# A hybrid decoder layer on one core: the first merge branch's weights in other buffers, its layer norm steps held back, and the memory stage's parts and stores in another order

## The chip, the cores and the metric

The kernel runs on one core of a Trainium2 chip. The metric is the time of one execution on the device, in microseconds (us). Before the change the median of three runs is 1679.34 us (1675.44 to 1679.78).

The engines are named as the profile names them: PE multiplies matrices (PEld loads its weights), DVE, ACT and POOL work element by element, and SP issues most of the transfers.

## The reference

The layer takes 1024 tokens of width 1024, in float32:

```
xn   = RMSNorm(x)
proj = xn @ w_in      # columns: attention q | 6 x k/v | gates | conv (2 x 512) | memory q (512) | 3 x 1024 merge gates
A: o_nsa  = sparse attention, 8 heads of 64: compressed blocks + top-16 selected blocks + window of 512
B: u      = silu(LayerNorm(causal depthwise conv, width 31, of a * sigmoid(ag)))
C: o_mem  = softmax(qm km^T / sqrt(128)) vm, 4 heads of 128 over 256 memory tokens
merged = sigmoid(g0) * (o_nsa @ w_nsa_out) + sigmoid(g1) * (u @ w_conv_out) + sigmoid(g2) * (o_mem @ w_mem_out)
h      = x + merged @ w_out
out    = h + (silu(hn @ w_gate) * (hn @ w_up)) @ w_down,   hn = RMSNorm(h)
```

With 1024 tokens the 16 selected blocks of 64 are all blocks, so branch A needs no gather: it is masked softmaxes over the compressed blocks, the keys and the window.

## The kernel before

**Products in parts.** Almost every product of float32 matrices is made of three. Each operand is split (`split`, lines 130 to 132) into a high part, which ACT casts (line 131), and a low part, the source less the high part, which DVE or, in places, POOL subtracts (line 132). `mm3` (line 153) then adds high by high, high by low and low by high into one bank of accumulators (`ps`, seven in three rings, and one bank `pf` for the gates). All of these are line 146 on PE.

**The stages in order.** The program is one sequence of stages for the same 1024 tokens:

1. Input norm, transposes, conv inputs, queries and compression (to about 262 us in the profile).
2. The memory stage. Eight units (2 head pairs by 4 tiles of 256 tokens) in `mem_attention`: scores and softmax (`mem_softmax`; POOL scales by the reciprocals at line 619), a transposition by 32 by 32 squares that goes through DRAM (`mem_squares` stores to `pd`, `mem_load` reads back), and the product with the values (`mem_out`). `mem_out` casts the read probabilities on ACT and subtracts on POOL, as one instruction of 128 by 1024, then makes 12 products of 256 columns for its two heads, and stores the result's parts to `md`. Between these stand the attention's query projections (`queries`). `square_queries` reads the stored queries back, scales them on POOL at line 356, transposes and stores them.
3. The K/V stage (its first PE transposes of keys stand at 387 us): eight projections (`wide_proj`), norm of the keys on DVE and ACT, and `keys(t)`, four PE transposes at line 696 and copies into place. `keys` runs one tile behind the projection. The last `mem_out` stands behind the first projection.
4. The attention (its last waits end at 806 us): for each of 8 token tiles and 2 groups, the scores of a step, masks and softmax, transposes of the probabilities on PE (line 932, and line 918 for the compressed part), their parts (ACT line 131, DVE line 132), and the products with the values. The selected blocks' probabilities go through `wd` in DRAM (line 855 stores 8 pieces per tile and group, line 869 reads).
5. The merge, three branches in the order memory, attention, convolution. For each branch four weight units `w` (512 by 256 columns, split into parts), and for each of 8 column blocks `d_` and 2 halves one bank of 12 products of 512 columns, which is multiplied by the sigmoid of a gate (`zz`, read from `zd`) and added to `acc`. `layer_norm` is a generator: each `next(steps)` runs a piece of the convolution's norm (sums of four, means by a product with `ones` at line 1023, squares, variances at line 1035, scaling, Silu and split), two pieces for each `d_`.
6. Output product, norm and feed-forward part.

**What fills PE.** The convolution's taps (line 445, on DVE) run along stages 2 and 3. The merge gates' projections (bank `pf`, weights in two buffers `fsl` with a staging buffer `fst` of their own) are fillers: the first 12 of 24 column blocks are free, and the others are tied one by one to matmuls of the attention. Fillers and taps have a later priority, so a scheduler puts them where the main line waits. What a merge weight needs: a staging buffer `st` (two in the kernel), a buffer for the parts, a load on SP's queue, a cast on ACT and a subtraction on DVE. `anyslab` hands out the part buffers by turns: three `wsl` and two `fsl`. In the attention the `wsl` buffers hold the squares that line 855 stores to `wd`, so a merge weight in one of them can only be cast once those stores have landed.

`follow(m, i)` orders instruction m behind i without data between them.

Of the kernel before, what the change touches and what calls it, by code (L numbers as in the profile page):

```python
# [8 lines left out]
F32 = mybir.dt.float32  # L9
# [3 lines left out]
OP = mybir.AluOpType  # L13
# [4 lines left out]
P = 128  # L18
S = 1024
D = 1024  # L20
NT = S // P
# [18 lines left out]
def hybrid_layer_kernel(  # L40
# [4 lines left out]
    nc = tc.nc  # L45
    x, mem, out = x[0], mem[0], out[0]
# [33 lines left out]
    turn = [0, 0, 0]  # L80
# [18 lines left out]
    def bank(shape, dt=F32, p=P, at=None):  # L99
        if at is None:  # L100
            turn[1] += 1
            at = order[turn[1] % len(order)]
        return psp[at].tile([p] + shape, dt, tag=f"ps{at}", name=nm("ps"))
# [26 lines left out]
    def split(hi, lo, src, eng=None):  # L130
        m = nc.scalar.copy(hi, src)  # L131
        return m, (eng or nc.vector).tensor_tensor(lo, src, hi.bitcast(F32), op=OP.subtract)  # L132
# [20 lines left out]
    def mm3(o, ah, al, bh, bl, start, stop):  # L153
        first = mm(o, ah, bh, start, False)
        mm(o, ah, bl, False, False)
        mm(o, al, bh, False, stop)
        return first
# [48 lines left out]
    def follow(m, i, why):  # L206
        tc.add_manual_dep(m.ins, i.name, ORDER, reason=why)
# [139 lines left out]
        nc.scalar.activation(stat, stat, AF.Sqrt, scale=stat.shape[2] / 512.0, bias=RMS_EPS)  # L347
        nc.vector.reciprocal(stat, stat)

    def square_queries(j, t, stat):  # L350

        h = stat.shape[2]
        raw, sq = t2([512]), t2([512])
        nc.sync.dma_start(raw, qraw[j, t])
        v = raw.rearrange("p (h d) -> p h d", h=h)
        nc.gpsimd.tensor_tensor(v, v, stat[:, t, :, None].to_broadcast([P, h, 512 // h]), op=OP.mult)
        if j == 0:
            nc.vector.transpose(sq.rearrange("p (c h s) -> p h c s", c=4, h=4),
                                raw.rearrange("p (h c s) -> p h c s", h=4, c=4))
            o = qt_m[t].rearrange("c r a x -> r c a x")  # L360
        else:
            for g in range(2):
                nc.vector.transpose(sq.rearrange("p (g c h s) -> p g h c s", g=2, c=2, h=4)[:, g],
                                    raw.rearrange("p (g h c s) -> p g h c s", g=2, h=4, c=2)[:, g])
            o = qt_n[t].rearrange("g c r a x -> r (g c) a x")
        for a in range(4):
            nc.sync.dma_start(o[:, :, a], sq[32 * a:32 * a + 32].rearrange("p (c x) -> p c x", c=4))
# [210 lines left out]
        ps = tok_proj(row_units(w_mem_kv, 512 + hp * 256), 0, mn)  # L578
        split(VM[:, 0, :, hp * 256:(hp + 1) * 256], VM[:, 1, :, hp * 256:(hp + 1) * 256], ps)

    msc, exps = float(P) ** -0.5, []

    def mem_qload(u):
        raw = t2([2, 4, 2, 32])
# [38 lines left out]
    def mem_squares(hp, tp, pm):  # L623
        T_ = t4([2, 4, 2, 2, 32])
        for tt in range(2):
            nc.vector.transpose(T_[:, :, :, :, tt, :].rearrange("p m c h s -> p h (m c) s"),
                                pm[:, tt].rearrange("p h (b s) -> p h b s", s=32))
        for a in range(4):
            nc.sync.dma_start(pd[hp, tp, :, :, :, a, :].rearrange("m c r x -> r (m c) x"),
                              T_[32 * a:32 * a + 32].rearrange("p m c h t s -> p (m c) (h t s)"))  # L630

    def mem_load(hp, tp):
        PT = slab([2, 2, 4, 2, 2, 32])
        nc.sync.dma_start(PT[:, 1].bitcast(F32).rearrange("p m a h t s -> p m (a h t s)"),
                          pd[hp, tp].rearrange("m c r a x -> (c r) m (a x)"))
        return PT

    def mem_out(hp, tp, PT):
        follow(split(PT[:, 0], PT[:, 1], PT[:, 1].bitcast(F32), nc.gpsimd)[0], exps[-1],
               "parts behind the next unit's exponentials")  # L640
        o = bank([2, 256])
        for h in range(2):
            hh = 2 * hp + h
            for mb in range(2):
                ph, pl = (PT[:, hl, mb, :, h].rearrange("p a t s -> p t a s") for hl in range(2))
                mm3(o[:, h, :].rearrange("p (t a s) -> p t a s", t=2, a=4), VM[:, 0, mb, hh * P:(hh + 1) * P],
                    VM[:, 1, mb, hh * P:(hh + 1) * P], ph, pl, mb == 0, mb == 1)
        om = [PT[:, hl, 0].rearrange("p a h t s -> p (a h t s)").rearrange("p (h t) -> p h t", h=2) for hl in range(2)]
        split(om[0], om[1], o)
        for hl in range(2):  # L650
            nc.sync.dma_start(md[2 * hp:2 * hp + 2, :, hl, tp * 256:(tp + 1) * 256].rearrange("h p t -> p h t"),
                              om[hl].bitcast(F32))

    def mem_attention(ws):

        raws, PT = [mem_qload(0), mem_qload(1)], {}
        QM = mem_queries(raws.pop(0))
        for u in range(8):
            if u < 6:
                raws.append(mem_qload(u + 2))  # L660
            pm = mem_softmax(u // 4, u % 4, QM)
            if u < 7:
                QM = mem_queries(raws.pop(0))
            mem_squares(u // 4, u % 4, pm)
            queries(ws, u, 1, rqn)
            if u > 1:
                mem_out(0 if u < 6 else 1, (u - 2) % 4, PT[u - 2])
            if u > 0:
                PT[u - 1] = mem_load((u - 1) // 4, (u - 1) % 4)
            if u == 3:  # L670
                stat_rms(rqn[:, 0:4])
            if u > 3:
                square_queries(1, u - 4, rqn)
        mem_out(1, 2, PT[6])
        return mem_load(1, 3)

    ws = [wide_unit(w_in, C_Q, u, alloc=slab if u == 3 else wslab) for u in range(4)]
    pt3 = mem_attention(ws)
    stat_rms(rqn[:, 4:8])


# [15 lines left out]
        for s in range(2):  # L697
            nc.vector.tensor_copy(key_cols(s, t), b[:, s].bitcast(F32))

    last = None  # L700
    for t in range(NT):
        if t < 4:
            square_queries(1, 4 + t, rqn)
        v = wide_proj(ws, t).rearrange("p (s a g d) -> p s a g d", s=2, a=2, g=2)
        if t == 0:
            mem_out(1, 3, pt3)
        kn = t2([2, 2, 64])
        heads_norm(v[:, :, 0], kn)
        nc.vector.tensor_tensor(kn, kn, gn[:, 2:4, None, :].to_broadcast([P, 2, 2, 64]), op=OP.mult)
        cat = t2([4, 2, 64], F32R)  # L710
        split(cat[:, :, 0, :], cat[:, :, 1, :], kn.rearrange("p s g d -> p (s g) d"))
        for s in range(2):
            split(VSW[s][:, t, :, 0:64], VSW[s][:, t, :, 64:128], v[:, s, 1])
        if last is not None:
            keys(t - 1, last)
        last = cat
    keys(NT - 1, last)


    with low(TAP):  # L720
# [342 lines left out]
    for n_, (br, wt) in enumerate(branches):  # L1063
        ins = nxt
        for dp in range(4):
            w = unit(wt[0, :, dp * 256:(dp + 1) * 256].rearrange("(k p) c -> p k c", p=P), [4, 256], alloc=anyslab)
            if dp == 2 and n_ == 0:
                nxt = [heads_in(k) for k in range(4)]
            elif n_ == 1:
                nxt = conv  # L1070
            for d_ in (2 * dp, 2 * dp + 1):
                for _ in range(2):
                    next(steps, None)
                wc = (d_ % 2) * P
                zz = t4([S])
# [2 lines left out]
                for half in range(2):  # L1078
# [14 lines left out]
                    if n_ == 2:  # L1093
# [2 lines left out]
                        m = MG[half][dp]  # L1096
                        split(m[:, 0, d_ % 2, :], m[:, 1, d_ % 2, :], a)


    def mg(hl, k, half, a, b):  # L1100
        return MG[half][k // 2][:, hl, k % 2, a:b]
# [375 lines left out]
```

## Time and profile before

| | us |
|---|---|
| median of 3 runs | 1679.34 |
| profiled execution, its own time | 1677.4 |
| span of the profiled execution | 1675.4 |
| PE busy in the span | 1637.0 |
| DVE busy | 1063.6 |
| ACT busy | 737.3 |
| POOL busy | 638.9 |
| mean granted clock of PE | 0.995 of full speed |

The span is what the trace covers; the 2.0 us between it and the execution's own time lie around it. "Busy" of PE includes matmuls that run at half the clock; the rows by windows give the granted clock as a share of full speed in their eighth column. The row of a group or a wait names engine, line and tiles; buffer numbers are left out there. In rows of the timeline a bracket gives the idle time ahead of an instruction and what ended it.

### The profile page before, as it was taken

The page shows a single profiled execution, that of the slowest core. Times are in us where ns is not written, and L with a number is a line of the kernel's source. Part 1 is how long each engine was busy: PE and PEld are TensorE (multiplying, and loading weights), DVE is VectorE, ACT ScalarE, POOL GpSimd, SP SyncE. Part 2 cuts the span into 40 slices and gives each one's busy share as a digit, 9 for nine tenths or more (in the row PEclk, how much of TensorE's full clock was granted, in tenths as well). Part 3 has the DMA queues.
Part 4 walks back from the last instruction along what each step waited for, and adds up shares of the span by engine and source line. Part 5 has one row for each costly group of instructions (what it writes and reads, how often), then busy time and mean ns, then how long its engine had stood idle before and what let it go on. Part 6 is the DMA issues. An engine that isn't in the chain of part 4 may idle for free.

```text
span 1675.4 us, 22491 instructions
## 1 busy us (share of the span) xinstructions
PE 1637.0 (98%) x7904; PEld 1368.2 (82%) x7904; DVE 1063.6 (63%) x1796; ACT 737.3 (44%) x1363; POOL 638.9 (38%) x551
## 2 busy tenths in 40 slices
PE   7999999999999999997999999999999999999999
PEld 6887898777888888886788888888888888888887
DVE  6279888798565665666585526865545555466655
ACT  6311344442676766575584324432223223233332
POOL 0010003451367767665115302465566766400000
PEclk9999999999999999999899999999999999999999
DMA  8134456663355555438654224233334445793763
GB/s 286 40 97 119 139 152 178 193 197 118 108 150 167 165 173 163 141 118 290 215 192 155 84 76 139 76 124 95 96 110 141 145 151 188 275 398 118 233 226 125
DMA packets 249430, 266.31 MB, mean 159 GB/s; under 512 B 24084, under 2 KB 173892, under 8 KB 247782
## 3 DMA queue, kind: packets, MB, share of 16 engines
q1 hardware_dynamic: 242406, 252.30, 47.4%
q10 hardware_dynamic: 6912, 12.59, 2.0%
q8 instruction: 62, 1.02, 0.2%
q14 instruction: 50, 0.41, 0.1%
HBM read 184.09 MB, written 80.74 MB: 158 GB/s over the span
## 4 chain that ended last, share of the span: by engine, by line
PE 89%; DVE 4%; DMA 3%; issue 2%; ACT 1%; SPq 1%; POOL 1%; DVEq 0%; POOLq 0%; ACTq 0%
PE ps L146 56%; PE pf L146 18%; PE ps L1411 11%; PE ps L932 2%; PE pf L1411 1%; DVE slab L445 1%; PE ps L236 1%; DVE wsl L132 1%; DMA t<-qraw 1%; SPq L855 0%; DMA wd<-wsl 0%; DMA gn<-in_nsa_qk_norm_dram 0%; POOL t L619 0%; DMA md<-slab 0%; PE ps L918 0%
## 5 line engine op out<-in xcount | busy, mean ns | idle before, releaser
L146 PE MATMUL ps<-slab,wsl 128*128 128x512 f32 (+1 forms) x1628 | 361.8, 381 | 0.0
L146 PEld LDWEIGHTS ps<-slab,wsl 128*128 128x128 f32 x1628 | 295.9, 188 | 58.9 <-issue 0.5
L146 PE MATMUL pf<-slab,fsl 128*128 128x512 f32 x1248 | 315.1, 395 | 1.7 <-ACT fz L1000 1.7
L146 PEld LDWEIGHTS pf<-slab,fsl 128*128 128x128 f32 x1248 | 229.0, 188 | 46.4 <-ACT fz L1000 2.8
L445 DVE SCALAR_TENSOR_TENSOR slab<-slab,cw 128x1019 f32<-128x1019 f32 (+16 forms) x120 | 167.4, 1399 | 1.4
L146 PE MATMUL ps<-slab,fsl 128*128 128x512 f32 x672 | 158.0, 391 | 0.0
L146 PE MATMUL ps<-slab,slab 128*128 128x512 f32 (+1 forms) x628 | 152.5, 378 | 5.1 <-POOL slab L132 2.2
L1307 DVE TENSOR_TENSOR t<-ps,t 128x512 f32<-128x512 f32 x130 | 88.7, 687 | 106.4 <-PE ps L146 105.1
L146 PE MATMUL ps<-wsl,slab 128*128 128x512 f32 (+1 forms) x690 | 148.7, 362 | 0.3 <-DVE slab L228 0.3
L146 PEld LDWEIGHTS ps<-slab,fsl 128*128 128x128 f32 x672 | 126.1, 188 | 27.4 <-issue 1.4
L146 PEld LDWEIGHTS ps<-slab,slab 128*128 128x128 f32 x628 | 112.2, 188 | 28.6 <-POOL slab L132 3.7
L146 PEld LDWEIGHTS ps<-wsl,slab 128*128 128x128 f32 x690 | 115.9, 189 | 19.3 <-DVE slab L228 0.5
L1411 PE MATMUL ps<-wsl 128*128 128x512 f32 x495 | 118.8, 389 | 0.0
L1411 PEld LDWEIGHTS ps<-wsl 128*128 128x128 f32 x495 | 93.0, 188 | 19.3
L132 DVE TENSOR_TENSOR wsl<-st,wsl 128x1024 fp32r<-128x1024 f32 x57 | 79.9, 1402 | 42.4 <-ACT wsl L131 33.5
L146 PE MATMUL ps<-slab,qt 128*128 128x384 f32 (+6 forms) x400 | 93.7, 338 | 1.0 <-ACT qt L131 0.7
L131 ACT CAST wsl<-st 128x1024 fp32r<-128x1024 f32 x58 | 61.0, 1051 | 75.7 <-PE ps L146 30.6
L146 PE MATMUL ps<-t,slab 128*128 128x256 f32 (+1 forms) x404 | 90.8, 326 | 2.9 <-DVE t L132 2.7
L131 ACT CAST wsl<-t 128x1024 fp32r<-128x1024 f32 x43 | 45.3, 1053 | 88.3 <-POOL t L128 35.0
L1320 POOL TENSOR_TENSOR t<-t,t 128x512 f32<-128x512 f32 x21 | 39.1, 1863 | 115.0 <-DVE t L1307 48.2
L1411 PE MATMUL ps<-fsl 128*128 128x512 f32 x330 | 80.2, 389 | 0.0
L132 POOL TENSOR_TENSOR slab<-slab,t 128x1024 fp32r<-128x1024 f32 (+1 forms) x28 | 62.6, 2238 | 43.6 <-ACT t L131 43.4
(253 smaller groups left out, 2772.5 us busy)
## 6 DMA issues: line engine op xcount, KB each, us to landing
t<-in_w_down_dram SPq DMA_DIRECT2D x70, 256.0 KB, 3.8
fst<-in_w_in_dram SPq DMA_DIRECT2D x24, 512.0 KB, 3.9
zd<-fz ACTq DMA_DIRECT2D x48, 256.0 KB, 2.6
slab<-wd SPq DMA_DIRECT2D x24, 512.0 KB, 5.0
t<-zd SPq DMA_DIRECT2D x24, 512.0 KB, 3.4
st<-in_w_gate_dram SPq DMA_DIRECT2D x22, 512.0 KB, 3.7
st<-in_w_up_dram SPq DMA_DIRECT2D x22, 512.0 KB, 4.3
ad<-t SPq DMA_DIRECT2D x44, 256.0 KB, 2.7
```

What stands on the lines that cost most here:

```text
L131: m = nc.scalar.copy(hi, src)
L132: return m, (eng or nc.vector).tensor_tensor(lo, src, hi.bitcast(F32), op=OP.subtract)
L146: m = nc.tensor.matmul(o, a, b, start=start, stop=stop)
L236: m = nc.tensor.transpose(b[:, kk, tt * P:(tt + 1) * P], js[tt][:, k * P:(k + 1) * P], ident)
L445: return nc.vector.scalar_tensor_tensor(acc[:, s:], u[:, :S - s], cw[:, ct, 30 - s:31 - s], acc[:, s:], op0=OP.mult, op1=OP.add)
L932: nc.tensor.transpose(b[:, j - j0, h, :], tiles[h][:, j * P:(j + 1) * P], ident)
L1307: nc.vector.tensor_tensor(o, a_, b_, op=OP.add)
L1320: nc.gpsimd.tensor_tensor(u4, u4, c22, op=OP.mult)
L1411: nc.tensor.matmul(B[t], a_, b_, start=start and k == 0 and j == 0, stop=k == FH - 1 and j == 2, skip_group_check=True)
```

## The change

Merge stage: the first two weight units of the first branch take the gates' buffers (`fslab`, with the staging buffer `fst`), the third and fourth the `wslab` buffers; later branches use `anyslab` as before, whose turn is advanced by four behind the loop, as four fewer units took a turn. In the first branch `layer_norm` gets 1, 1, 1, 1, 2, 2, 3, 3 pieces in the eight column blocks, where each got 2.

Memory stage: in `mem_out` the subtraction on POOL is two instructions of 128 by 512, and the products are ordered so that the four with the probabilities' high part of both key blocks come ahead of those with the low part (for each head; the number of products is the same 12). The result's stores follow the last squares' stores to `pd`, and the queries' scaling follows the parts. The last two `mem_out` stand in the K/V stage behind projections 0 and 2 (one did before, behind projection 0), and `keys` runs two tiles behind the projection.

```diff
-    def square_queries(j, t, stat):
+    def square_queries(j, t, stat, after=None):
...
-        nc.gpsimd.tensor_tensor(v, v, stat[:, t, :, None].to_broadcast([P, h, 512 // h]), op=OP.mult)
+        m = nc.gpsimd.tensor_tensor(v, v, stat[:, t, :, None].to_broadcast([P, h, 512 // h]), op=OP.mult)
+        if after is not None:
+            follow(m, after, "scaled behind the memory values' parts")
...
     def mem_out(hp, tp, PT):
-        follow(split(PT[:, 0], PT[:, 1], PT[:, 1].bitcast(F32), nc.gpsimd)[0], exps[-1],
+        follow(nc.scalar.copy(PT[:, 0], PT[:, 1].bitcast(F32)), exps[-1],
                "parts behind the next unit's exponentials")
+        for mb in range(2):
+            part = nc.gpsimd.tensor_tensor(PT[:, 1, mb], PT[:, 1, mb].bitcast(F32), PT[:, 0, mb].bitcast(F32),
+                                           op=OP.subtract)
...
-            for mb in range(2):
-                ph, pl = (PT[:, hl, mb, :, h].rearrange("p a t s -> p t a s") for hl in range(2))
-                mm3(o[:, h, :].rearrange("p (t a s) -> p t a s", t=2, a=4), VM[:, 0, mb, hh * P:(hh + 1) * P],
-                    VM[:, 1, mb, hh * P:(hh + 1) * P], ph, pl, mb == 0, mb == 1)
+            ov = o[:, h, :].rearrange("p (t a s) -> p t a s", t=2, a=4)
+            for hl, mb in ((0, 0), (0, 1), (1, 0), (1, 1)):
+                p_ = PT[:, hl, mb, :, h].rearrange("p a t s -> p t a s")
+                mm(ov, VM[:, 0, mb, hh * P:(hh + 1) * P], p_, hl == 0 and mb == 0, hl == 1 and mb == 1)
+                if hl == 0:
+                    mm(ov, VM[:, 1, mb, hh * P:(hh + 1) * P], p_, False, False)
...
+            follow(nc.sync.dma_start(
+                md[2 * hp:2 * hp + 2, :, hl, tp * 256:(tp + 1) * 256].rearrange("h p t -> p h t"),
+                om[hl].bitcast(F32)), stored[-1], "outputs behind the squares")
+        return part.ins
...
-                square_queries(1, u - 4, rqn)
-        mem_out(1, 2, PT[6])
-        return mem_load(1, 3)
+                square_queries(1, u - 4, rqn, part)
+        return [PT[6], mem_load(1, 3)]
...
-        if t == 0:
-            mem_out(1, 3, pt3)
+        if t in (0, 2):
+            mem_out(1, 2 + t // 2, rest.pop(0))
...
-        if last is not None:
-            keys(t - 1, last)
-        last = cat
-    keys(NT - 1, last)
+        cats.append((t, cat))
+        if t > 1:
+            keys(*cats.pop(0))
+    for c in cats:
+        keys(*c)
...
-            w = unit(wt[0, :, dp * 256:(dp + 1) * 256].rearrange("(k p) c -> p k c", p=P), [4, 256], alloc=anyslab)
+            w = unit(wt[0, :, dp * 256:(dp + 1) * 256].rearrange("(k p) c -> p k c", p=P), [4, 256],
+                     alloc=anyslab if n_ else fslab if dp < 2 else wslab)
...
-                for _ in range(2):
+                for _ in range(2 if n_ else (1, 1, 1, 1, 2, 2, 3, 3)[d_]):
                     next(steps, None)
...
+    turn[0] += 4
```

How the scheduler moves instructions is seen in each engine's order. The first place is PE at the end of the attention. `ps_1207` and `ps_1254` are the value sums of the last two pairs of tile and group, `ps_1255` holds transposed compressed probabilities, `ps_1257`, `ps_1259`, `ps_1261` transposed ones, and `ps_1435` and `ps_1440` to `ps_1443` are merge banks. Before:

```order
L146 MATMUL ps_1207_6219<-slab_1206_6216,slab_386_2684 128x512
L932 MATMUL ps_1257_6458<-identr_107,slab_1221_6282 128x128 x4
L918 MATMUL ps_1255_6449<-identr_107,t2_1220_6281 64x128 x2
L146 MATMUL ps_1207_6219<-t4_1251_6426,slab_386_2684 128x512
L932 MATMUL ps_1259_6470<-identr_107,slab_1221_6282 128x128 x4
L932 MATMUL ps_1261_6482<-identr_107,slab_1221_6282 128x128 x4
L146 MATMUL ps_1207_6219<-slab_1206_6216,slab_386_2684 128x512
L146 MATMUL ps_1207_6219<-t4_1251_6426,slab_386_2684 128x512
L146 MATMUL ps_1207_6219<-slab_1206_6216,slab_386_2684 128x512
L146 MATMUL ps_1207_6219<-t4_1231_6321,slab_386_2684 128x512 x2
L932 MATMUL ps_1263_6494<-identr_107,slab_1221_6282 128x128 x4
L146 MATMUL ps_1254_6448<-t2_1256_6454,vcmp_136 128x512
```

After:

```order
L927 MATMUL ps_1255_6457<-identr_107,t2_1220_6289 64x128 x3
L941 MATMUL ps_1257_6466<-identr_107,slab_1221_6290 128x128 x4
L146 MATMUL ps_1443_8177<-slab_1186_6153,fsl_1438_8137 128x512 x3
L146 MATMUL ps_1443_8177<-slab_1187_6155,fsl_1438_8137 128x512 x3
L146 MATMUL ps_1443_8177<-slab_1218_6285,fsl_1438_8137 128x512 x3
L146 MATMUL ps_1443_8177<-slab_1219_6287,fsl_1438_8137 128x512 x3
L146 MATMUL ps_1207_6227<-t4_1251_6434,slab_385_2671 128x512
L941 MATMUL ps_1259_6478<-identr_107,slab_1221_6290 128x128 x4
L146 MATMUL ps_1207_6227<-slab_1206_6224,slab_385_2671 128x512
L146 MATMUL ps_1207_6227<-t4_1251_6434,slab_385_2671 128x512
L146 MATMUL ps_1207_6227<-slab_1206_6224,slab_385_2671 128x512
L146 MATMUL ps_1207_6227<-t4_1231_6329,slab_385_2671 128x512 x2
```

Twelve products of a merge bank, `ps_1443`, now stand between the transposes `ps_1257` and the value product that needs `t4_1251`; 24 more, of `ps_1440` and `ps_1441`, stand ahead of the first row shown, among the value products of `ps_1207`. Before, the first merge product (`ps_1435`) stood seventeen rows behind the first row shown.

The second place is ACT in the same stretch: `fsl_` and `wsl_` are casts of merge weights, `t4_` those of probabilities for the value products. Before:

```order
L131 CAST t4_1240_6363<-ps_1239_6362 128x512
L131 CAST fsl_1438_8130<-st_1437_8128 128x1024
L815 ACTIVATE slab_1241_6374,sm_1243_6376<-slab_1241_6374,sm_1242_6375 128x1024
L131 CAST t4_1231_6321<-t4_1231_6321 128x512
L131 CAST t4_1251_6426<-slab_1206_6216 128x1024
L131 CAST t4_1258_6459<-ps_1257_6458 128x512
L131 CAST wsl_1448_8211<-st_1447_8209 128x1024
L131 CAST t4_1260_6471<-ps_1259_6470 128x512
L131 CAST fsl_1460_8307<-st_1459_8305 128x1024
L131 CAST t4_1262_6483<-ps_1261_6482 128x512
L131 CAST wsl_1470_8387<-st_1469_8385 128x1024
```

After:

```order
L131 CAST t4_1238_6359<-ps_1237_6358 128x512
L131 CAST t4_1240_6371<-ps_1239_6370 128x512
L824 ACTIVATE slab_1241_6382,sm_1243_6384<-slab_1241_6382,sm_1242_6383 128x1024
L131 CAST t4_1231_6329<-t4_1231_6329 128x512
L131 CAST wsl_1460_8306<-st_1459_8304 128x1024
L131 CAST wsl_1470_8391<-st_1469_8389 128x1024
L131 CAST t4_1251_6434<-slab_1206_6224 128x1024
L131 CAST t4_1258_6467<-ps_1257_6466 128x512
L131 CAST t4_1260_6479<-ps_1259_6478 128x512
L912 COPY t2_1252_6449<-ps_1207_6227 64x512
L131 CAST t2_1256_6462<-ps_1255_6457 64x512
L131 CAST t4_1262_6491<-ps_1261_6490 128x512
```

The casts of the fourth memory weight (`wsl_1460`) and of the next branch's first weight (`wsl_1470`), behind each other, now stand ahead of the parts `t4_1251` and `t4_1258`; before, these parts stood ahead of `wsl_1448`, and `wsl_1470` came after `t4_1262`.

The third place is POOL in the memory stage. Line 132 on `slab_` and line 644 are `mem_out`'s parts, line 356 the queries' scaling, and lines 619 and 621 the softmax's scaling. Before:

```order
L132 TENSOR_TENSOR slab_300_2134<-slab_300_2134 128x1024
L356 TENSOR_TENSOR t2_331_2334<-t2_331_2334,rqn_134 128x512
L619 TENSOR_SCALAR t4_317_2239<-t4_317_2239,sm_321_2243 128x256 x4
L132 TENSOR_TENSOR t4_324_2270<-t2_301_2136,t4_324_2270 128x256 x2
L132 TENSOR_TENSOR slab_315_2232<-slab_315_2232 128x1024
L356 TENSOR_TENSOR t2_348_2442<-t2_348_2442,rqn_134 128x512
```

After:

```order
L644 TENSOR_TENSOR slab_300_2135<-slab_300_2135 128x512 x2
L621 TENSOR_SCALAR t4_317_2241<-t4_317_2241,sm_321_2245 128x256 x4
L132 TENSOR_TENSOR t4_324_2272<-t2_301_2137,t4_324_2272 128x256 x2
L644 TENSOR_TENSOR slab_315_2234<-slab_315_2234 128x512 x2
L356 TENSOR_TENSOR t2_331_2337<-t2_331_2337,rqn_134 128x512
```

The one subtraction of 128 by 1024 is two of 128 by 512, and `t2_331`'s scaling has moved from ahead of the softmax scaling `t4_317` to behind the parts `slab_315`, which it stood ahead of.

More of the change, by code (lines that the diff above doesn't have):

```diff
@@ L579, in hybrid_layer_kernel @@
         split(VM[:, 0, :, hp * 256:(hp + 1) * 256], VM[:, 1, :, hp * 256:(hp + 1) * 256], ps)
-    msc, exps = float(P) ** -0.5, []
+    msc, exps, stored = float(P) ** -0.5, [], []
     def mem_qload(u):
@@ L628, in mem_squares @@
         for a in range(4):
-            nc.sync.dma_start(pd[hp, tp, :, :, :, a, :].rearrange("m c r x -> r (m c) x"),
-                              T_[32 * a:32 * a + 32].rearrange("p m c h t s -> p (m c) (h t s)"))
+            stored.append(nc.sync.dma_start(pd[hp, tp, :, :, :, a, :].rearrange("m c r x -> r (m c) x"),
+                                            T_[32 * a:32 * a + 32].rearrange("p m c h t s -> p (m c) (h t s)")).ins)
     def mem_load(hp, tp):
@@ L650, in mem_out @@
         for hl in range(2):
-            nc.sync.dma_start(md[2 * hp:2 * hp + 2, :, hl, tp * 256:(tp + 1) * 256].rearrange("h p t -> p h t"),
-                              om[hl].bitcast(F32))
+            follow(nc.sync.dma_start(
+                md[2 * hp:2 * hp + 2, :, hl, tp * 256:(tp + 1) * 256].rearrange("h p t -> p h t"),
+                om[hl].bitcast(F32)), stored[-1], "outputs behind the squares")
+        return part.ins
     def mem_attention(ws):
@@ L666, in mem_attention @@
             if u > 1:
-                mem_out(0 if u < 6 else 1, (u - 2) % 4, PT[u - 2])
+                part = mem_out(0 if u < 6 else 1, (u - 2) % 4, PT[u - 2])
             if u > 0:
@@ L672, in mem_attention @@
             if u > 3:
-                square_queries(1, u - 4, rqn)
-        mem_out(1, 2, PT[6])
-        return mem_load(1, 3)
+                square_queries(1, u - 4, rqn, part)
+        return [PT[6], mem_load(1, 3)]
     ws = [wide_unit(w_in, C_Q, u, alloc=slab if u == 3 else wslab) for u in range(4)]
-    pt3 = mem_attention(ws)
+    rest = mem_attention(ws)
     stat_rms(rqn[:, 4:8])
@@ L698, in keys @@
             nc.vector.tensor_copy(key_cols(s, t), b[:, s].bitcast(F32))
-    last = None
+    cats = []
     for t in range(NT):
```

## The prediction

> **What bounds the kernel now.** I read the page's busy rows first, then the busy time by windows.
>
> ```profile
> span 1675.4 us, 22491 instructions
> PE 1637.0 (98%) x7904; PEld 1368.2 (82%) x7904; DVE 1063.6 (63%) x1796; ACT 737.3 (44%) x1363; POOL 638.9 (38%) x551
> 262.00:380.00 118.00, 111.12 (x546) 91.03 (x544) 103.19 (x119) 54.88 (x121) 54.14 (x52) 1.00 0.67 199
> 380.00:790.00 410.00, 399.70 (x2159) 341.48 (x2159) 263.21 (x858) 254.40 (x632) 243.94 (x257) 1.00 0.51 157
> 1065.00:1462.00 397.00, 397.00 (x1753) 328.93 (x1752) 211.52 (x243) 118.48 (x152) 244.42 (x162) 1.00 0.44 142
> 1462.00:1676.00 214.00, 209.67 (x926) 173.35 (x924) 131.10 (x145) 75.63 (x72) 5.53 (x5) 1.00 0.64 223
> ```
>
> The columns are the window, its length, and busy time of PE, PEld, DVE, ACT and POOL; then granted clock, DMA share and GB/s. PE is the bound. The change takes no matmul away and adds none, so it can win only PE's idle time (1675.4 − 1637.0 = 38.4 us) and time in which a busy PE ran at a lower clock. Of the idle time, 6.9 us (118.00 − 111.12) lie in the memory stage and the projections behind it, 10.3 us in the K/V stage and the attention, 4.3 us in the last window, which the change doesn't touch. The merge, from 830 us, shows 100%.
>
> The second view is the end of the attention, in pieces of 5 us:
>
> ```profile
> 775.00:780.00 5.00, 3.50 (x23) 2.79 (x22) 4.86 (x17) 5.00 (x11) 4.09 (x3) 1.00 0.35 128
> 780.00:785.00 5.00, 4.14 (x25) 3.22 (x25) 3.29 (x8) 2.52 (x4) 2.46 (x3) 1.00 0.89 276
> 785.00:790.00 5.00, 1.76 (x7) 0.82 (x7) 1.17 (x3) 3.19 (x7) 4.42 (x6) 0.89 0.87 226
> 790.00:795.00 5.00, 1.04 (x5) 1.04 (x6) 4.91 (x3) 1.59 (x3) 2.22 (x1) 0.50 0.90 300
> 795.00:800.00 5.00, 3.32 (x10) 1.91 (x8) 1.76 (x3) 2.65 (x4) 0.00 (x0) 0.50 0.62 197
> 800.00:805.00 5.00, 3.45 (x15) 3.35 (x16) 2.16 (x4) 1.53 (x3) 0.00 (x0) 0.50 0.55 150
> 805.00:810.00 5.00, 5.00 (x30) 4.48 (x28) 1.45 (x3) 2.16 (x5) 3.64 (x2) 0.91 1.02 376
> ```
>
> Two things add up. PE is idle for 1.50 + 0.86 + 3.24 + 3.96 + 1.68 + 1.55 = 12.8 us from 775 to 805. And its clock is halved for about 17 us: 0.89 in the third row means 1.1 us at half clock, then 15 us, then 0.9 us (0.91). The busy time in those 17 us is 1.04 + 3.32 + 3.45 and 0.9 us at the end, 8.7 us, half of it lost: 4.4 us. This place costs **17.2 us**, more than any other that the change touches. What it waits for is in the chain of waits there (start, length, what):
>
> ```profile
> 786.82 2.16 DMA wd<-wsl
> 789.02 1.05 ACT wsl L131
> 790.09 3.22 DVE wsl L132
> 793.33 4.41 DMA st<-in_w_nsa_out_dram
> 797.89 1.05 ACT wsl L131
> 798.97 1.23 DVE wsl L132
> 800.19 0.59 DVE t L904
> 800.81 0.69 DVE t L132
> 801.55 3.57 PE ps L146 x14
> ```
>
> A merge weight may be cast only after the last squares have landed (2.16 us), its cast and its subtraction stand on ACT and DVE ahead of the parts that PE waits for, and PE has no other work, since the merge's first bank stands behind them in its order.
>
> **The change, part by part: the merge.** Loads, casts and subtractions stay the same in number; they move. Two weights go to buffers that no store to DRAM holds, so three banks of the first branch (12 + 12 + 12 matmuls) come into PE's order ahead of the wait. A matmul of this size takes 397.00 / 1753 = 0.226 us, from the fifth row of the first fence, so 36 are 8.2 us of work for 12.8 us of idle time.
>
> They don't fill it all. In the new order of ACT the casts `wsl_1460` and `wsl_1470` stand ahead of `t4_1251` and `t4_1258`, and both need a buffer from which the squares are still being stored. SP's queue issues those stores behind the loads of these two weights, and the second of the loads needs the staging buffer that the third memory weight's subtraction frees. That subtraction stands on DVE where the row at 778.41 below stood, so I take the stores' landing where it was, 789.0 us.
>
> ```profile
> 778.41 1.22 DVE L132 TENSOR_TENSOR wsl<-st,wsl 128x1024 fp32r<-128x1024 f32 x1
> 790.09 3.21 DVE L132 TENSOR_TENSOR wsl<-st,wsl 128x1024 fp32r<-128x1024 f32 x1 [2.16 <-ACT wsl L131]
> 789.88 2.35 POOL L132 TENSOR_TENSOR slab<-slab,t 128x1024 fp32r<-128x1024 f32 x1
> 786.63 0.58 ACT L131 CAST t<-ps 128x512 fp32r<-128x512 f32 x1
> 796.64 0.69 DVE L132 TENSOR_TENSOR t<-ps,t 128x512 fp32r<-128x512 f32 x1 [1.60 <-ACT t L131]
> 787.98 0.66 PE L932 MATMUL ps<-identr,slab 128*128 128x128 f32 x4 [0.71 <-DVE t L132]
> 801.55 0.80 PE L146 MATMUL ps<-t,vcmp 128*128 128x512 f32 x1 [3.05 <-DVE t L132]
> ```
>
> From 789.0: two casts of 1.05 us to 791.1; the cast of `t4_1251`, of the same shape, to 792.1; `t4_1258` (0.58) to 792.7. On DVE one subtraction beside POOL's (3.21 us beside the 2.35 us of POOL, 1.22 us alone: the two delay each other) to 793.3, the next (1.22) to 794.5, `t4_1258` (0.69) to 795.2. PE, which reaches the transposes `ps_1257` at about 788 (784.3 before, plus 24 matmuls, less 2.1 us of idle time that they fill), has the 12 of `ps_1443` to 791, one matmul at 792.1, and then waits for a bank of transposes until 795.2. The next round costs 0.58 + 0.69 us, to some 797.3, and the compressed part's two copies and subtractions bring the product with `vcmp` to about 798.7. Before, it started at 801.55 (last row): 2.9 us earlier. In the order 7.7 us more work stands ahead of it than before: the 36 matmuls of 8.2 us, less about 0.5 us of others that moved behind. That is 10.6 us. Behind 801.55 the 17 us at half clock still had 4.4 us to run (805.9 − 801.55), so a full clock saves another 2.2 us: 12.8 us. If the clock is halved again for part of this, some 2 us of that goes. I take **11 us**. From above it is bounded by 17.2 us, all there is. From below: both subtractions at 3.21 us (2.0 us later), the stores landing 2.7 us later (should half of the 24 matmuls' 5.4 us delay what they wait for), and a half clock for as long as before (2.2 us and 1.5 us more): 12.8 − 8.4, some 4 us.
>
> Of the clock, the row 785 to 790 shows a fall at 788.9, when PE had just had 0.2 us of its longest wait. [...]
>
> The norm's pieces held back cost nothing: two of 16 pieces of the first branch go to the second, and in the merge PE shows no idle time, with DVE busy in 52 of 80 us from 985 to 1065 us.
>
> ```profile
> 985.00:1065.00 80.00, 80.00 (x387) 66.84 (x386) 52.13 (x77) 39.55 (x78) 14.41 (x9) 1.00 0.39 122
> ```
>
> The third branch starts behind 32 banks of 12 matmuls (32 × 2.7 = 87 us) from the point where the norm began, so two pieces of a few us each are covered. If the cover is gone, PE waits for about those two pieces, 3 to 7 us.
>
> **The memory stage.**
>
> ```profile
> 321.02 3.37 POOL L132 TENSOR_TENSOR slab<-slab 128x1024 fp32r<-128x1024 f32 x1
> 324.44 1.59 PE L146 MATMUL ps<-slab,slab 128*128 128x256 f32 x11 [0.80 <-POOL slab L132]
> 335.84 3.35 POOL L132 TENSOR_TENSOR slab<-slab 128x1024 fp32r<-128x1024 f32 x1
> 339.25 0.98 PE L146 MATMUL ps<-slab,slab 128*128 128x256 f32 x6 [1.42 <-POOL slab L132]
> L1092 POOL TENSOR_TENSOR slab<-slab,t x32: 1280/1294/2209, 865.9 to 947.1; 128x512 f32<-128x512 f32 x32
> PE ps L696 <- DVE t L132: 2.4, 1, 2.4
> ```
>
> In two units PE waits for POOL's subtraction, 0.80 and 1.42 us. Halved (1.29 us each by the row of the same shape, up to 2.2 beside DVE), and with four products that need no low part ahead, the first half is there before PE needs it: 2.2 us. The queries' scaling (line 356) is held behind these parts; it has waited for its own load anyway, and what it feeds is needed in the attention. The result's stores go behind the squares' stores on SP: `md` is read only at the merge. Other short waits here come from casts and loads; I count 1 us for them. The longest wait, 2.4 us for the keys' low part at the first transposes, should stay: before `keys`, DVE has as much to do, and it is what is late.
>
> ```profile
> 370.00:380.00 10.00, 9.04 (x45) 7.16 (x43) 10.00 (x14) 2.02 (x3) 1.51 (x1) 1.00 0.73 190
> 380.00:390.00 10.00, 7.59 (x40) 6.06 (x41) 9.86 (x14) 1.80 (x7) 3.57 (x2) 1.00 0.47 155
> 390.00:400.00 10.00, 10.00 (x48) 8.31 (x47) 10.00 (x18) 2.12 (x7) 2.39 (x1) 1.00 0.41 132
> ```
>
> DVE is full here (third busy column: 10.00, 9.86, 10.00). One more `mem_out` comes into this stretch: one subtraction of a 128x512 bank (0.69 us), and POOL's 3.4 us beside DVE, which then pays up to 2.0 us (3.21 − 1.22). Each sits where PE has fillers or the next projection, so I take a gain of **3 us**, with bounds of +7 (the 6.9 us of idle time) and −5 (2.7 us for each of two `mem_out`).
>
> **Sum.** 1677.4 (the profiled execution: 1675.4 and 2.0 around it) − 11 − 3 = 1663.4 us. The runs' median is 1679.34, 1.9 us above that execution; with half of it I predict **1664 us**.
>
> **The rivals.**
>
> *The wait only moves (A).* The order of ACT speaks for it: two casts that must wait for the stores now stand ahead of two parts, where one stood behind both. Then PE runs out at 791, the clock stays half as before, and the tail gains its lower bound of 4 us, the memory stage 2: about 1672. Against it: the 36 matmuls are real work that moves ahead of the wait.
>
> *The K/V stage becomes later (B), slower.* DVE is the bound from 370 us on. If the two moved `mem_out` and the keys two tiles behind hold up the first scores, DVE loses 2 × (0.69 + 2.0) = 5.4 us, and the last keys come one projection (24 matmuls of 0.226, 5.4 us) later. It decides from the point where this 10.8 us exceeds the tail's gain; with A's 4 us the time is 1677.4 + 10.8 − 4, about 1684. Against it: the attention has fillers to use meanwhile, and these are spent in the end whatever the order.
>
> *It is given back (C).* In the merge PE is full but the loads of gates and outputs, the norm and the weights share queues that now have another order; a gain of 14 us in front means that PE asks for all later weights 14 us sooner. If loads set the pace there, the time stays at 1676 to 1678. Against it: the DMA share in the merge's windows is 0.39 (985 to 1065) and 0.44 (1065 to 1462).
>
> **Chances.** Forecast (1656 to 1669) 0.62; A 0.18; B 0.09; C 0.11. A measurement here can tell about 0.3%, 5 us, from no change: faster means below 1674.3. All of the forecast and most of A (0.14) lie there: 0.76. The rest of A and C with what falls within 5 us: 0.15. B: 0.09. The range reaches from all of the tail and 7 us of the memory stage (1677.4 − 24.2, of which I take 1655) to 1676, which takes in A and leaves B and part of C out.
>
> **What would show it.** The tail's step is right if the rows from 775 to 805 show idle PE below 7 us and if merge products (`ps<-slab,fsl`) stand ahead of the product with `vcmp`; it is wrong if PE still waits more than 5 us for DVE's `t` of line 132 there. The clock's step: no pieces at 0.50, or fewer than three. ACT's order is the cause if the chain there runs `wd<-wsl`, two casts, then `t`. The memory stage's step: no wait for POOL's parts, and 2.4 us still at the keys' transposes. It is wrong as a whole if the merge's rows no longer show 100%, or if the attention's first scores start later.

## The result

The changed kernel's median is **1665.86 us** (1665.55 to 1667.3, 4 runs), against 1679.56 us for the kernel before (1675.44 to 1680.67, 4 runs): a ratio of **0.9925**, with an interval of 0.9907 to 0.9942; the medians differ by 13.7 us. The prediction was 1664 us, in a range of 1655 to 1676. The profiled execution took 1666.06 us, with a span of 1664.2 us and a mean granted clock of 1.000 (0.995 before).

The page and the windows of the profile after, to be read beside those of before (columns as there):

```profile
span 1664.2 us, 22505 instructions
PE 1636.1 (98%) x7904; PEld 1366.2 (82%) x7904; DVE 1060.1 (64%) x1796; ACT 737.2 (44%) x1363; POOL 655.9 (39%) x559
262.00:380.00 118.00, 112.00 (x552) 91.95 (x552) 103.03 (x120) 53.07 (x120) 68.05 (x61) 1.00 0.69 205
775.00:780.00 5.00, 4.50 (x33) 3.78 (x31) 4.86 (x18) 4.97 (x10) 3.23 (x3) 1.00 0.87 326
780.00:785.00 5.00, 4.20 (x21) 2.97 (x21) 4.68 (x9) 3.44 (x8) 4.29 (x3) 1.00 0.64 185
785.00:790.00 5.00, 5.00 (x28) 4.22 (x27) 0.18 (x1) 0.86 (x3) 4.34 (x5) 1.00 0.93 278
790.00:795.00 5.00, 3.98 (x20) 2.82 (x18) 3.04 (x3) 3.42 (x4) 1.14 (x2) 1.00 0.86 257
795.00:800.00 5.00, 2.54 (x13) 1.77 (x13) 2.00 (x4) 2.23 (x4) 1.52 (x1) 1.00 0.78 279
800.00:805.00 5.00, 4.87 (x31) 4.44 (x32) 1.46 (x3) 2.33 (x4) 1.21 (x1) 1.00 0.64 210
```

At the end of the attention, from 775 to 805 us, PE is idle for 0.50 + 0.80 + 0.00 + 1.02 + 2.46 + 0.13 = 4.9 us, where it was 12.8 us, and the clock stays at 1.00, where it was halved for 17 us (4.4 us lost, by the prediction's estimate half of the busy time there; the product with `vcmp` took 0.80 us at half clock and takes 0.50 us after). Together that is 12.3 us. In the memory stage's window PE's idle time went from 6.9 to 6.0 us.

Counting matmuls from the start, by their ends, places the gain. The two traces have the same 7904. The 1200th stands 0.4 us later than before, the 1600th (in the memory stage) 1.7 us earlier, the 2800th (in the attention) 0.7 us later, the 4000th, at 784 us, 1.1 us later. The 4400th, in the merge, stands 11.1 us earlier, and so does the last one. So in these two executions the whole difference arises between 784 and 873 us, and what the memory stage won was gone again within the attention. (The two executions differ by 11.3 us, the medians by 13.7: the one profiled before was 2 us faster than the median of its runs.)

The chain of waits at the end of the attention, after (start, length, what):

```profile
783.03 7.73 DMA wd<-wsl
790.87 0.67 ACT wsl L131
...
791.82 1.05 ACT wsl L131
792.87 0.95 ACT t L131
...
793.89 2.64 POOL slab L132
796.58 1.46 PE ps L146 x5
798.06 0.59 ACT t L912
798.67 0.68 DVE t L913
799.39 0.70 DVE t L132
800.13 1.58 PE ps L146 x10
```

It is the chain that the prediction named: the squares land, two casts of merge weights, then the parts. Two things are new in it. The squares land at 790.9 us, not at 789.0, and the cast of `t4_1251` has a subtraction behind it, on POOL, which I had not counted.

### The profile page after: what moved, and what is told of

Its sections match the earlier page's. It is cut to its first block, busy times and chain, and to the rows that moved or that the text cites. A ratio compares the mean times of both kernels' runs of the same rounds, so it can differ in the third digit from the quotient of the medians.

```text
span 1664.2 us, 22505 instructions
## 1 busy us (share of the span) xinstructions
PE 1636.1 (98%) x7904; PEld 1366.2 (82%) x7904; DVE 1060.1 (64%) x1796; ACT 737.2 (44%) x1363; POOL 655.9 (39%) x559
## 3 DMA queue, kind: packets, MB, share of 16 engines
q8 instruction: 62, 1.02, 0.3%
## 4 chain that ended last, share of the span: by engine, by line
PE 70%; DVE 4%; DMA 3%; POOL 2%; issue 2%; ACT 1%; SPq 1%; DVEq 0%; POOLq 0%; ACTq 0%
PE ps L146 41%; PE pf L146 15%; PE ps L1423 11%; DVE slab L447 1%; DMA wd<-wsl 1%; PE ps L941 1%; PE pf L1423 1%; POOL slab L644 1%; PE ps L236 0%; SPq L864 0%; POOL t L132 0%; DVE t L628 0%; POOL slab L132 0%; DMA slab<-wd 0%; ACT t L615 0%
## 5 line engine op out<-in xcount | busy, mean ns | idle before, releaser
L146 PE MATMUL pf<-slab,fsl 128*128 128x512 f32 x1236 | 309.7, 394 | 3.6 <-ACT fz L1009 3.3
```

Of the source, the lines that this page charges most:

```text
L146: m = nc.tensor.matmul(o, a, b, start=start, stop=stop)
```

## The experiments

Each kernel's ratio is to runs of the kernel before on the same chip, whose median was 1677.6 to 1678.4 us in these sessions (1679.56 for the changed kernel's).

| run | what it is | median, us | ratio (interval) |
|---|---|---|---|
| changed kernel | all | 1665.86 | 0.9925 (0.9907 to 0.9942) |
| e1_merge | merge part alone | 1666.74 | 0.9926 (0.9913 to 0.9940) |
| e2_memory | memory part alone | 1680.04 | 1.0012 (1.0003 to 1.0020) |
| e3_no_hold | changed, norm not held back | 1675.26 | 0.9978 (0.9968 to 0.9987) |
| e4_hold_only | changed, weights in old buffers | 1671.72 | 0.9958 (0.9943 to 0.9974) |
| e9_mean_pf | e3, means' bank elsewhere | 1665.62 | 0.9927 (0.9912 to 0.9942) |
| e5_lag1 | changed, keys one tile behind | 1667.99 | 0.9942 (0.9929 to 0.9956) |
| e6_place | changed, memory outputs at old places | 1665.62 | 0.9925 (0.9909 to 0.9942) |
| e7_one_part | changed, one subtraction, old order | 1669.57 | 0.9959 (0.9944 to 0.9974) |
| e10_parts_only | merge part, halves and order | 1674.52 | 0.9982 (0.9973 to 0.9991) |
| e12_no_scaling_hold | changed, scaling not held | 1673.88 | 0.9983 (0.9972 to 0.9995) |
| e11_stores | changed, two loads behind stores | 1664.20 | 0.9919 (0.9904 to 0.9933) |
| e13_merge_stores | e1 with e11's edit | 1664.60 | 0.9926 (0.9912 to 0.9940) |

### Which part carries the gain: e1 and e2

e1 is the kernel before with the merge's three places alone (the weights' buffers, the pieces of the norm, the turn); e2 is the changed kernel without them.

> The kernel before with the merge stage's part alone (weights in the gates' buffers, norm's pieces held back); the memory stage as before. The prediction's theory, with the sizes of the profile after: the tail is worth 12 us and the memory stage 1 to 3, so this is 10 to 12 us below before (about 1668). Rival, that the memory stage's order is needed for it or carries the larger part: less than 6 us below before.

> The memory stage's part alone, the merge as before. The prediction's theory: 3 us below before; by the idle time of the profile after (2.1 us less in the memory stage, 1.4 us more in the attention) 1 us. Rival, that it carries the gain: over 6 us below. The waits at the end of the attention (over 5 us) and the half clock should stay in both.

e1 is 11.7 us below before, with the same ratio as the whole change. e2 is not faster; its interval lies just above 1. The memory stage's edits sum up to no gain. In e2 the waits at the end of the attention are those of before:

```profile
775.00:805.00 30.00, 16.78 (x85) 12.77 (x84) 19.02 (x36) 16.40 (x29) 13.14 (x11) 0.81 0.68 219
```

13.2 us idle and a mean clock of 0.81.

### Buffers or held-back pieces: e3 and e4

e3 gives the norm two pieces in each column block again, e4 takes the weights' buffers back; all else is the changed kernel.

```diff
# e3
-                for _ in range(2 if n_ else (1, 1, 1, 1, 2, 2, 3, 3)[d_]):
+                for _ in range(2):
# e4
-                     alloc=anyslab if n_ else fslab if dp < 2 else wslab)
+                     alloc=anyslab)
...
-    turn[0] += 4
```

> The changed kernel with two pieces of the norm in each column block again, the weights still in the gates' buffers. Theory of the prediction (the buffers carry the tail's gain, the held-back pieces cost and win nothing): the time of the changed kernel, within 2 us. Rival (the held-back pieces are what lets merge products stand ahead of the last value products; without them PE's order has no merge product ahead of the product with vcmp): 6 to 12 us above the changed kernel, with over 8 us of idle time at the end of the attention.

> The changed kernel with the weights in the old buffers and the norm's pieces held back. Theory of the prediction (the buffers carry it): most of the gain is gone, 8 to 12 us above the changed kernel. Rival (the pieces carry it; PE's order has 36 merge products between the last transposes here too): within 4 us of the changed kernel.

The prediction's account failed here. Measured from e2, which has neither edit, the buffers alone win 4.8 us (1680.04 − 1675.26) and the held-back pieces alone 8.3 us (1680.04 − 1671.72); the two add up to 13.1 of the whole 14.2 us. e3 came out as its rival said; e4, 5.9 us above the changed kernel, lies between its two. PE's waits in e3, the engine's view (total, times, longest), and its rows of the timeline:

```profile
PE ps L941 <- DVE t L132: 8.2, 2, 7.8
786.68 0.51 PE L146 MATMUL ps<-t,slab 128*128 128x512 f32 x1
795.00 1.11 PE L941 MATMUL ps<-identr,slab 128*128 128x128 f32 x4 [7.81 <-DVE t L132]
```

No merge product stands in this gap: in e3's order they all follow the product with `vcmp`, though their weights are ready. The timeline of e4:

```profile
785.06 4.84 PE L146 MATMUL ps<-slab,fsl 128*128 128x512 f32 x20
...
791.93 2.55 PE L146 MATMUL ps<-slab,fsl 128*128 128x512 f32 x10
...
800.85 0.79 PE L146 MATMUL ps<-t,vcmp 128*128 128x512 f32 x1 [4.76 <-DVE t L132]
```

Here the 36 merge products fill the gap without the new buffers, out of the second weight, `fsl_1438`, which `anyslab` had put into an `fsl` buffer anyway. What is left is a wait of 4.76 us ahead of `vcmp`, for parts that stand behind a further weight's cast and subtraction.

### Why the pieces matter: e9

The norm's means are summed by a product with `ones` whose accumulators, `pm_`, come from the rings of banks that the merge's products use too. That product needs the convolution's rows back from DRAM, which are read behind the squares' last stores. With two pieces in each block, `pm_` is taken ahead of the third block's bank, and the banks handed out later in the same ring have to wait for it. All 36 products are of the third and fourth block, whose banks come behind `pm_` in that order. e9 is e3 with one word changed:

```diff
-            pm_ = bank([512])
+            pm_ = fbank([512])
```

> As e3 (two pieces of the norm in each column block, weights in the gates' buffers), but the accumulators of the norm's means are taken from the gates' bank and not from the rings that the merge's banks share. Theory after e3 and e4: what the held-back pieces do is move the means' accumulators, which wait for the convolution's rows from DRAM, behind the first merge banks in those rings; then PE's order has 36 merge products ahead of the product with vcmp here too, and the time is that of the changed kernel within 2 us (9 us below e3). Rival: the pieces' additions and subtractions on DVE, which stay early here, are what costs; then the time stays within 3 us of e3.

1665.62 us: with two pieces in each block, the same time as the changed kernel. In the order of e9 the 36 merge products stand ahead of the product with `vcmp` as they do in the changed kernel; the norm's additions stand on DVE where e3 has them, row for row. So it is the bank, not DVE's work. Its windows:

```profile
785.00:790.00 5.00, 5.00 (x27) 4.27 (x26) 1.02 (x4) 2.01 (x4) 3.17 (x5) 1.00 1.00 303
790.00:795.00 5.00, 5.00 (x29) 4.13 (x29) 3.38 (x3) 3.27 (x4) 2.79 (x2) 1.00 0.73 208
795.00:800.00 5.00, 2.74 (x16) 1.95 (x15) 2.60 (x4) 2.23 (x4) 0.89 (x1) 1.00 0.91 331
```

### The memory stage taken apart: e5, e6, e7, e10, e12

```diff
# e6: the last two memory outputs at their old places
-        return [PT[6], mem_load(1, 3)]
+        mem_out(1, 2, PT[6])
+        return [mem_load(1, 3)]
...
-        if t in (0, 2):
-            mem_out(1, 2 + t // 2, rest.pop(0))
+        if t == 0:
+            mem_out(1, 3, rest.pop(0))
# e5: the keys one tile behind
-        if t > 1:
+        if t > 0:
             keys(*cats.pop(0))
# e7: one subtraction, products in the old order
-        for mb in range(2):
-            part = nc.gpsimd.tensor_tensor(PT[:, 1, mb], ...)
+        m, part = split(PT[:, 0], PT[:, 1], PT[:, 1].bitcast(F32), nc.gpsimd)
...
-            for hl, mb in ((0, 0), (0, 1), (1, 0), (1, 1)):
+            for mb in range(2):
+                ph, pl = (PT[:, hl, mb, :, h].rearrange("p a t s -> p t a s") for hl in range(2))
+                mm3(...)
# e12: the scaling not held (e10: e5, e6 and e12 together, and the stores of md not held)
-                square_queries(1, u - 4, rqn, part)
+                square_queries(1, u - 4, rqn)
```

> The changed kernel with the last two memory outputs at their old places. If their new place causes the waits of 0.92 us and 1.66 us for POOL's parts (which the kernel before didn't have there), these go; by the prediction's sum the time changes by less than 3 us. Rival (the K/V stage gained by the move: 1.24 us of waiting for the keys' parts after, 2.41 before): that wait is back at 2.4 us.

> The changed kernel with the memory outputs' low part as one subtraction on POOL and the products in the old order. The prediction's step (halves and products that need only the high part take away 2.2 us of waits): the waits of 0.8 and 1.4 us for POOL's parts at about 322 and 338 us are back, and the time is 1 to 3 us above the changed kernel. Rival: what is won there is given back in the attention, and the time is the same within 1 us.

> The changed kernel's merge, and of the memory stage only the two halves on POOL and the order of the products; the scaling of the queries, the stores, the places of the last memory outputs and the keys as before. e7 showed that the halves and the order win 3.7 us where the other memory edits are there. Theory (the other edits cost as much as the halves win, and the two add up): 2 to 4 us below the changed kernel. Rival (the halves only take back what the held-back scaling and stores cost; on the old stage they win what the waits of 0.8 and 1.4 us allowed, and the attention gives it back): within 1 us of the changed kernel.

> The changed kernel without the order that holds the queries' scaling on POOL behind the memory values' parts. Theory (this order costs in the attention, whose first queries come later): 1 to 3 us below the changed kernel. Rival: the same within 1 us, or slower by up to 2 us because the scaling, which waits for its load, stands ahead of the parts on POOL again.

> The changed kernel with the keys one tile behind the projection again. If the second tile took away 1.2 us of waiting for the keys' parts (2.41 before, 1.24 after), the time is 1 us above the changed kernel and that wait is back at 2.4 us. Rival (it delays the first scores, and the attention's 2.7 us of idle time, 1.1 more than before, come from that): 1 to 2 us below.

e6 changes nothing (1665.62 us), although its waits are others: the one for POOL that ends at 380 us goes from 1.67 to 0.66 us, the one at 363 us grows from 0.92 to 1.44 us, one of 1.29 us for ACT appears at 376 us, and the keys wait for 0.54 us, not 2.4. The time stayed within the 3 us that were expected; neither expectation about the waits held. e5's median is 2.1 us above the changed kernel's (0.9942 against 0.9925, with intervals that overlap); the keys wait for 1.24 us in it, so the second tile was not what halved that wait.

e7, at 1669.57 us, looks as the prediction wanted it: halves and order are worth 3.7 us where the other memory edits are in. But in e7 the waits for POOL's parts at 322 and 338 us are not back. What is new is a wait of 2.98 us at 345 us, for ACT's queries, one of 1.79 us at 371 us, and a clock at half for 3.41 us twice, from 316.8 and from 347.6 us. e10 and e12 go the other way altogether: with halves and order but without the held-back scaling the kernel is 8 us *slower* than the changed one, which neither expectation of either run had. Both show one wait of 4.35 us at 339 us. PE's timeline there in e10, with a copy on ACT, and then after:

```profile
338.58 0.39 PE L146 MATMUL pf<-slab,fsl 128*128 128x512 f32 x1
343.32 2.50 PE L146 MATMUL ps<-slab,t 128*128 128x256 f32 x8 [4.36 <-ACT t L131]
344.39 0.61 ACT L1010 COPY fz<-pf 128x512 f32<-128x512 f32 x1
```

```profile
338.54 0.59 ACT L1009 COPY fz<-pf 128x512 f32<-128x512 f32 x1
339.18 5.73 PE L146 MATMUL pf<-slab,fsl 128*128 128x512 f32 x24 [0.98 <-ACT fz L1009]
344.75 1.12 PE L146 MATMUL ps<-slab,t 128*128 128x256 f32 x8
```

The memory scores need the same thing in both, the cast of the next queries, which comes behind the exponentials and ends at 343.0 us after and at 343.6 us in e10. In the changed kernel a whole bank of 24 gate products (5.7 us) stands in that place; in e10 and e12 PE has none there and waits, and from about 342 us its clock is halved for 6.8 us. The kernel before has the same 24 products at 340.7 us. They need the bank `pf` empty, and the copy that empties it stands ahead of the exponentials on ACT in the changed kernel (338.5 us) and before (337.9 us), behind them in e10 (344.4 us) and e12 (344.7 us).

So an edit in this stage also moves a bank of fillers, whatever it does to the wait that it is aimed at. How much of the 8 us comes from that is not shown. By counting matmuls e10 falls from 0.6 to 7.8 us behind the changed kernel at this place, gets 4.8 us of it back by the 2000th matmul and ends 5.7 us behind. e12 falls behind by as much and loses more later, with a wait of 2.15 us at 404 us and two further falls of the clock; but its profiled execution took 1680.27 us, 6.4 us above its median, and doesn't stand for its usual time. No run moves a filler bank by itself.

### The stores ahead of the loads: e11 and e13

In the profile after, SP's queue holds the squares' stores behind two loads, of the fourth memory weight and of the next branch's first one, each of which waits for a staging buffer:

```profile
779.98 0.38 SPq L271 DMA_DIRECT2D st<-in_w_mem_out_dram  x1
780.80 0.38 SPq L271 DMA_DIRECT2D st<-in_w_nsa_out_dram  x1
781.24 8.10 SPq L864 DMA_DIRECT2D wd<-wsl  x8
```

The squares themselves were ready at 775.9 us, when DVE's transposition ended. e11 orders the two loads behind the last store (`held`, a new argument of `unit`, is passed to `follow`), which also moves their casts on ACT behind the value parts; e13 puts the same into e1.

```diff
+                     held=(squares[-1], None) if (n_, dp) in ((0, 3), (1, 0)) else (None, None))
```

> The changed kernel, with the loads of the fourth memory weight and of the next branch's first weight ordered behind the last stores of the squares on SP's queue; their casts then come behind the last value parts on ACT too. Theory: of the changed kernel's 4.7 us of idle time at the end of the attention, 0.38, 0.71, 0.85 and 1.67 us hang on the two casts that wait for the stores to land and on the stores that wait behind the loads; they go down by some 3 us together, and the time is 2 to 3 us below the changed kernel. Rival: the later weights are missed in the merge, which then shows idle time: no gain or up to 5 us slower.

> The kernel before with the merge's part of the change and the two loads behind the squares' stores (e11's edit); the memory stage as before. e1 showed that the merge's part alone has the whole gain, e11 that its edit is worth some 2 us. Theory (the memory stage's edits sum up to nothing, the tail's add up): 1664 to 1665, within 1.5 us of e11. Rival (the memory stage's edits are worth 1 us or more once the tail is clear): 1666 or above.

e11 takes 1664.20 us (1663.79 to 1664.49), 1.4 us less than e6 and e9 in the same session (1665.62 each), where 2 to 3 us were expected; the intervals of the ratios overlap, so the gain rests on the traces as much as on the times. The stores and the tail's windows in e11:

```profile
776.02 6.83 SPq L868 DMA_DIRECT2D wd<-wsl  x8
790.00:795.00 5.00, 5.00 (x29) 4.15 (x28) 0.69 (x1) 0.90 (x3) 2.84 (x2) 1.00 0.01 2
795.00:800.00 5.00, 3.55 (x24) 2.74 (x23) 2.75 (x4) 2.00 (x5) 0.00 (x0) 1.00 0.10 26
900.00:985.00 85.00, 84.52 (x374) 69.65 (x373) 37.66 (x49) 28.29 (x45) 22.44 (x16) 1.00 0.26 81
```

From 775 to 805 us PE is now idle for 2.8 us (4.9 after). By counting matmuls e11 is 2.7 us ahead of the changed kernel over the tail; 0.8 us go back in the merge, 0.5 us of them in a wait for a weight's cast (last row), which is the rival's mechanism at a small size. e13, without any edit in the memory stage, takes 1664.60 us (1662.18 to 1666.97), as its theory said: the memory stage's edits are not needed. That e13 is faster than e1 the times don't show, since its ratio is e1's (0.9926); in its trace, which is of the fastest of its five executions, it gains 3.1 us on e1 over the tail, by counting matmuls.

## Why the prediction was right, and where it was not

**The size of the tail.** Predicted 11 us (12.8 with a full clock), measured 12.3 us in the trace, 11.7 us in e1. The step from the landing of the squares through two casts was right in kind. The product with `vcmp` came at 800.1 us, not at 798.7: the stores landed 1.9 us later, and the subtractions on DVE took 2.36 us for both, not 3.21 and 1.22, with POOL idle from 790.0 to 793.9 us; but POOL's own 2.63 us, behind the late cast of `t4_1251`, held up the second half of that tile's products (0.85 us of waiting). That the product came 1.4 us late and that the 2 us kept for a half clock weren't needed offset each other: that the number is so near is luck in part.

**The clock.** The 2 us that I kept for a half clock were an estimate of mine that no run shows: after, the clock stays at 1.00 in every row from 775 to 805 us, with 1.67 us as the longest wait. How near a fall was, the waits don't tell: in e1 PE is idle for 0.71 us from 790 to 795 us and for 1.64 us from 795 to 800, against 1.02 and 2.46 us after, and the clock was at half for 3.4 us (0.66 in the row from 795).

**The cause of the tail's gain** was wrong. The prediction's step "two weights go to buffers that no store to DRAM holds, so three banks come into PE's order ahead of the wait" gives the buffers what the held-back pieces do, and "the norm's pieces held back cost nothing" is the step that failed: they are worth 8.3 us (e2 to e4), the buffers 4.8 us (e2 to e3). I took the 36 products from the new order, where both edits were already in, and didn't ask which of them had moved the products. The rows that I showed could have told me: the products of `ps_1443` read `fsl_1438`, and that weight is cast into an `fsl` buffer in ACT's order before the change as well. That the sum came out right rests on the order, not on the reason; that is luck. What the buffers do by themselves is smaller, and its cause stays open: from 775 to 805 us PE is idle nearly as long in e3 as in e2 (12.4 and 13.2 us), with a longer longest wait (7.8 and 5.3 us), but its clock is at half for 6.83 us and not for twice that.

**The memory stage.** Predicted 3 us, measured none: e1 has the changed kernel's ratio without it, and e2 is 1.6 us slower than before. The step "the first half is there before PE needs it: 2.2 us" held where it was stated and failed beside it. Of the two waits of 0.80 and 1.42 us, 0.56 us is left, at 322 us. But two units that had no such wait before have one now, at 363 and 380 us, so that PE's wait for these parts is 3.1 us in all, where it was 2.2:

```profile
322.17 2.03 PE L146 MATMUL ps<-slab,slab 128*128 128x256 f32 x11 [0.56 <-POOL slab L644]
362.87 0.39 PE L146 MATMUL ps<-slab,slab 128*128 128x256 f32 x1 [0.92 <-POOL slab L644]
379.76 1.10 PE L146 MATMUL ps<-slab,slab 128*128 128x256 f32 x7 [1.67 <-POOL slab L644]
PE ps L146 <- POOL slab L644: 3.1, 3, 1.7
332.31 4.49 POOL L644 TENSOR_TENSOR slab<-slab 128x512 fp32r<-128x512 f32 x2
331.62 4.03 DVE L447 SCALAR_TENSOR_TENSOR slab<-slab,cw 128x1017 f32<-128x1017 f32 x2
```

Beside DVE's taps (last two rows) each half took 2.25 us, at the upper end that I had named, and the sum of two, 4.5 us, is longer than the one subtraction before (3.35 us). The wait at the keys' transposes, which I had left in place, went from 2.4 to 1.3 us; but it is 1.56 us in e1, whose memory stage is that of before, so most of this is not the edits'.

The sum also left out what an order does to a busy PE. From the 1200th to the 3900th matmul PE is idle for 10.95 us after and 11.58 us before, but busy for 509.11 us and 507.77 us. That is 1.3 us more for the same number of matmuls, and in e5, with the keys one tile behind again, it is 507.82 us. So what the waits gave, busy time took twice over; why the matmuls take longer there no run shows.

**The rivals.** A, the wait that only moves, described the place rightly (the chain after is A's) and its price wrongly. B and C did not come: from the 4400th matmul on the two traces differ by the same 11.14 us to the end.

## What to carry to other kernels

Before crediting an edit with work that an order shows in a gap, undo the edit alone and look whether the work is still there; two edits had arrived together here, and the plainer one was not the cause. In rings of accumulators that are handed out in the order of the program, a small product that waits for late data holds up every later user of its ring: give it a bank of its own, or ask for it later (9.6 us here, e3 to e9). And a store that others wait for shouldn't stand in a queue behind loads that wait for buffers (2.7 us over the tail in e11's trace).

## What the runs showed of the hardware

The time at half clock, by the traces' records of the granted clock (those in the span's first 30 us and at its end left aside), was 17.1 us before, 13.7 us in e2, 6.8 us in e3, in e4 and in e7, 3.4 us in e1, 10.2 us in e10, 20.5 us in e12, and none in the changed kernel, e5, e6, e9, e11 or e13. Before, the clock fell at 788.88 us, 0.2 us into the wait of 5.32 us; after, the wait of 1.67 us passed at full clock. What makes the clock fall, no run shows.

DVE's taps and POOL's subtraction took longer beside each other: a tap took 1.26 us with POOL idle and 2.0 us beside the subtraction, and a half of the subtraction 2.25 us beside the taps and 1.27 us without a tap beside it (two in 2.54 us). The timeline after has for each without the other:

```profile
325.40 1.26 DVE L447 SCALAR_TENSOR_TENSOR slab<-slab,cw 128x1018 f32<-128x1018 f32 x1
348.00 2.54 POOL L644 TENSOR_TENSOR slab<-slab 128x512 fp32r<-128x512 f32 x2
```

By these rows two taps and two halves are 2 × 1.26 + 2 × 1.27 = 5.1 us of work one after the other; side by side the four took some 5.2 us, from 331.62 to 336.80. Halving the subtraction bought an earlier first half here, and no time on POOL: the two halves took 4.49 us beside two taps, the one subtraction before 3.35 us beside parts of two.
